# Two-step transposes on VectorE and ScalarE in a hybrid decoder layer on one core

## The chip, the cores and the metric

The kernel runs on one core of one Trainium2 chip, in one launch. The metric is the device time of that launch in microseconds (us). The kernel before takes 1019.77 us, the median of 3 runs (1019.71 to 1019.9).

## The reference, cut to what matters

One decoder layer on 256 tokens with D = 2048, all in float32. What the change touches is the end of it:

```python
def mixer_layer(x, p_i, ...):
    h = rmsnorm(x, norm_g)
    proj = h @ w_in                                   # q, k, v, gate paths, merge gates
    ya = moba_attention(...); yb = swa_attention(...); yc = rglru_branch(...)
    y = jnp.stack([ya * silu(ga), yb * silu(gb), yc * silu(gc)], axis=2)
    y_d = einsum('bsnc,ncd->bsnd', y, w_br)           # each branch to D columns
    gates = sigmoid(mg)
    merged = einsum('bsnd,bsnd->bsd', gates, y_d)     # gated sum of the three branches
    x = x + merged @ w_out
    x = x + sigmoid(rmsnorm(x, ple_norm_g) @ w_pg) * (p_i @ w_pp)
    return x
# output: rmsnorm(x, final_norm_g)
```

A matrix product on TensorE (PE) contracts over partitions, so its left side has to lie feature-major: features on the 128 partitions, tokens along the row. `merged` and the new `x` come out of a product token-major, and both are left sides of the next product (`w_out`, then `w_pg`). They must be transposed on the way.

## The kernel before, in words

**Three products for one.** Every float32 value that goes through PE is split into a rounded high part and the rest (`_hi`, `_lo`). `mm3` (L115 to L119) makes a product out of three matmuls: high by high (L117), high by the weights' low part (L118), low by high (L119).

**Weights.** A weight tile is 128 by 1024 float32 (512 KB). SyncE fetches it into one of 4 raw buffers (`r_*`, L96); `split` (L99) has ScalarE (ACT) cast it into `wh_*` (L111) and VectorE (DVE) subtract that from it into `wl_*` (L112), each in one of 4 buffers. A tile of a 512-column product holds two of the 128-feature steps `k`, and PE makes 2 steps x 2 token halves x 3 = 12 matmuls of 512 columns from it.

**Stages at the end.** `merge` (L634) runs for the three branches in turn; for the last (`bi == 2`, names ending in b) it goes over four column blocks `n`. For each, the gate columns are projected (`ps_in`, 8 weight tiles), then the branch output (`ps_brb`, 4 tiles); DVE multiplies (L647) and adds to `merged` (L648); then `turn` (L620) makes the block feature-major. After that `w_out` runs over four blocks (`ps_out`, 8 tiles each); DVE adds `x` (L673), ACT takes the squares (L676), and `turn` makes the new `x` feature-major as `x2T`, scaled by the norm's gain. Last, `w_pg` runs over blocks of 512 (`ps_pg`; names pg0, pg1, pg2, 8 tiles each) and two of 256 columns; ACT takes the sigmoid from PSUM (L711).

**The transposes.** `turn` has PE transpose 128 by 128 squares against an identity into a PSUM tile `tp_*` (L626), 8 squares for a block of 512 columns and 256 tokens. ACT and DVE then split straight out of that PSUM tile (`split_act`, L179 and L180, or `split_scaled`, L192 and L193). Eight blocks are turned: m0 to m3 of `merged` and x20 to x23 of `x`.

**What sets the order.** A scheduler orders the instructions of each engine from a simulated timeline when the kernel is built; `high_priority` (L105) pulls the splitting of weights ahead of other work, and `tc.issue_after` puts an instruction behind a named one on its engine. On the chip, each engine then works through its own list strictly in that order. A product into PSUM has two buffers (`ps_mm`), small scratch tiles (`temp`) four.

Of the kernel before, what the change touches and what calls it, by code (L numbers as in the profile page):

```python
# [11 lines left out]
F32 = mybir.dt.float32  # L12
# [25 lines left out]
NEG = -1e30  # L38
SLOT = 2112
WPAD = 64  # L40
WOFF = 32
RV = 384

# [2 lines left out]
def trunk(ctx: ExitStack, tc: tile.TileContext, x, xt, p, table, onehot, maskv, w_in, sinks, conv, w_ri, vec, fin, w_br,  # L46
# [23 lines left out]
    def temp(name):  # L70
        return small.tile([P, 4, SEQ], F32, tag="tmp", name=name, bufs=4)
# [14 lines left out]

    raws = {}
    casts = []
    loads = []
    first_parts = {}  # L90

# [7 lines left out]
    def split(name, off):  # L99
        r, pieces = raws.pop(name)  # L100
        hi = wsp.tile([P, WT + WPAD], F32R, tag="whi", name=f"wh_{name}")[:, off : off + WT]
        lo = wsp.tile([P, WT + WPAD], F32R, tag="wlo", name=f"wl_{name}")[:, off : off + WT]
        n = WT // pieces
        part = first_parts.pop(name, None)
        with tc.high_priority(offset=LEAD if part is None else 0):  # L105
            for j in range(pieces):
                c = slice(j * n, (j + 1) * n)
                if part:
                    part(j, pieces)
                with tc.issue_after(casts[-1]) if part else nullcontext():  # L110
                    casts.append(nc.scalar.copy(hi[:, c], r[:, c]).ins)  # L111
                nc.vector.tensor_tensor(lo[:, c], r[:, c], hi[:, c].bitcast(F32), op=ALU.subtract)  # L112
        return hi, lo

    def mm3(ps, a, b, first, last):  # L115
        (ah, al), (bh, bl) = a, b
        nc.tensor.matmul(ps, ah, bh, start=first, stop=False)  # L117
        nc.tensor.matmul(ps, ah, bl, start=False, stop=False)  # L118
        nc.tensor.matmul(ps, al, bh, start=False, stop=last)  # L119

    def weights_of(src, row, name, sub, off=0):
        held = {}

        def get(k):
            s = k // sub
            if s not in held:
                key = f"{name}_{s}"
                if key not in raws:
                    fetch(src, row + s, key)
                held[s] = split(key, off)  # L130
            return held[s], k % sub

        return get

    def matrix_psum(name):
        return ps_mm.tile([P, NH, CW], F32, tag="mm", name=f"ps_{name}")

    def project(act, src, row, name, cw=CW, weights=None, half=None, hooks={}):
        nk = len(act)
        if half is None:  # L140
            ps = matrix_psum(name).rearrange("p h c -> p (h c)")
        else:
            ps = aux(f"ps_{name}_{half}")
        get = weights or weights_of(src, row, name, WT // cw)
        for k in range(nk):
            w, kk = get(k)
            if k in hooks:
                with tc.issue_after(casts[-1]):
                    hooks[k]()
            c = slice(kk * cw, (kk + 1) * cw)  # L150
            for h in range(NH) if half is None else [half]:
                o = h * cw if half is None else 0
                q = slice(h * P, (h + 1) * P)
                mm3(ps[:, o : o + cw], [t[:, q] for t in act[k]], [t[:, c] for t in w],
                    k == 0 and o % CW == 0, k == nk - 1 and (half is not None or (o + cw) % CW == 0))
        return ps if half is not None else ps[:, : NH * cw].rearrange("p (h c) -> p h c", h=NH)

    def project_turned(row, name):
        ps = matrix_psum(name)
# [460 lines left out]
    def turn(u, n, src, name, gain=None):  # L620
        for j in range(0, 4, 2):
            pt = aux(f"tp_{name}{n}{j}")
            for i in range(2):
                for h in range(NH):
                    c = n % 2 * CW + (j + i) * P
                    nc.tensor.transpose(pt[:, i * SEQ + h * P : i * SEQ + (h + 1) * P], src[:, h, c : c + P], ident)  # L626
            k = n % 2 * 4 + j
            if gain is None:
                split_act(u, k, 2, pt)
            else:  # L630
                for i in range(2):
                    split_scaled([t[:, cols(k + i)] for t in u], pt[:, cols(i)], gain[:, 4 * n + j + i : 4 * n + j + i + 1])

    def merge(z, bi, br):  # L634
        if bi == 0:
            merged.extend(wide(block(f"merged{h}")) for h in range(2))
        for n in range(4):
            sg = token_major(temp(f"sg_{br}{n}"))
            ps = in_chunk()
            for h in range(NH):  # L640
                nc.scalar.activation(sg[:, h, :], ps[:, h, :], AF.Sigmoid, scale=rs1[:, h : h + 1])
            py = project(act_of(z), w_br, (bi * 4 + n) * KB * CW // WT, f"br{br}{n}")
            dst = merged[n // 2][:, :, half_cols(n)]
            if bi == 0:
                nc.vector.tensor_tensor(dst, py, sg, op=ALU.mult)
                continue
            nc.vector.tensor_tensor(sg, py, sg, op=ALU.mult)  # L647
            (nc.vector if bi == 2 else nc.gpsimd).tensor_tensor(dst, dst, sg, op=ALU.add)  # L648
            if bi == 2:
                if n % 2 == 0:  # L650
                    mT.append(unit(f"m{n // 2}"))
                turn(mT[n // 2], n, merged[n // 2], "m")

    steps = branch_c()
    next(steps)
# [14 lines left out]
    for n in range(4):  # L670
        ps = project(act_of(*mT), w_out, n * KD * CW // WT, f"out{n}")
        sl = xr[n // 2][:, :, half_cols(n)]
        nc.vector.tensor_tensor(sl, ps, sl, op=ALU.add)  # L673
        junk = token_major(temp(f"jy{n}"))
        for h in range(NH):
            nc.scalar.activation(junk[:, h, :], sl[:, h, :], AF.Square, accum_out=sq2[:, h, n : n + 1])  # L676
        turn(x2T[n // 2], n, xr[n // 2], "x2", ple_g)
    tot = const.tile([P, NH], F32, name="tot")
    rs2 = const.tile([P, NH], F32, name="rs2")
    nc.vector.reduce_sum(tot, sq2, axis=AX.X)  # L680
# [13 lines left out]
    for n in range(5):  # L694
        cw = CW if n < 3 else HW
        at = n * CW if n < 3 else 3 * CW + (n - 3) * HW
        b, lc = at // BW, slice(at % BW, at % BW + cw)
        if n < 3:
            parts = project(act_of(*x2T), w_pg, n * KD * CW // WT, f"pg{n}")
        elif n == 3:  # L700
            parts = project(act_of(*x2T), w_pgt, 0, f"pg{n}", cw=HW)
        y = token_major(temp(f"y{n}"))
        junk = token_major(temp(f"jz{n}"))
        ws = weights_of(w_pgt, KD * HW // WT, f"pg{n}", WT // HW)
        for h in range(NH):
            if n == 4:
                ps = project(act_of(*x2T), None, 0, f"pg{n}", cw=HW, weights=ws, half=h)[:, :HW]
            else:
                ps = parts[:, h, :]
            yh, xh = y[:, h, :cw], xr[b][:, h, lc]  # L710
            nc.scalar.activation(yh, ps, AF.Sigmoid, scale=rs2[:, h : h + 1])  # L711
            nc.vector.tensor_tensor(yh, yh, pps[b][:, h, lc], op=ALU.mult)
            nc.vector.tensor_tensor(xh, xh, yh, op=ALU.add)
            if n < 4:
                nc.scalar.activation(junk[:, h, :cw], xh, AF.Square, accum_out=sq3[:, h, n : n + 1])
                nc.gpsimd.tensor_tensor(xh, xh, fg[:, at : at + cw], op=ALU.mult)
                continue
            t, r = tot3[:, h : h + 1], rs3[:, h : h + 1]
            nc.vector.tensor_tensor_reduce(junk[:, h, :cw], xh, xh, op0=ALU.mult, op1=ALU.add, scale=1.0,
                                           scalar=0.0, accum_out=t)  # L720
            nc.vector.tensor_scalar(t, t, 1.0 / D, part[:, h : h + 1], op0=ALU.mult, op1=ALU.add)
            nc.gpsimd.tensor_tensor(r, t, half_c[:, :1], op=ALU.pow)
            nc.vector.tensor_tensor(xh, xh, fg[:, at : at + cw], op=ALU.mult)
            for eng, c0, c1 in ((nc.sync, 0, BW), (nc.scalar, BW + CW, D), (nc.sync, BW, BW + CW)):
                sl = xr[c0 // BW][:, h, c0 % BW : c0 % BW + c1 - c0]
                if eng is nc.sync:
                    nc.vector.tensor_scalar_mul(sl, sl, r)
                else:
                    nc.scalar.activation(sl, sl, AF.Copy, scale=r)
                eng.dma_start(out[h * P : (h + 1) * P, c0:c1], sl)  # L730
        if n == 3:
            nc.vector.reduce_sum(part, sq3, axis=AX.X)
            nc.vector.tensor_scalar(part, part, 1.0 / D, EPS, op0=ALU.mult, op1=ALU.add)
# [78 lines left out]
```

## Time and profile before

| what | value |
|---|---|
| median of 3 runs | 1019.77 us |
| the profiled execution's own time | 1020.7 us |
| its span on the core | 1018.6 us |
| PE busy, share of the span | 1007.2 us, 99% |
| PE weight loads (PEld) | 857.7 us, 84% |
| DVE busy | 653.6 us, 64% |
| ACT busy | 555.2 us, 55% |
| granted PE clock | 0.998 of full |
| share of the chain that ended last | PE 96%, DMA 2%, issue 1% |

A busy time is the union of an engine's instructions. Matmuls overlap in the pipeline, so what PE needs for a stretch is read from the distances between the starts of its instructions, not from the mean time of one. The chain of waits is followed back from the last instruction; an engine with 96% of it sets the end.

### The profile page before, as it was taken

What the parts mean: (1) busy time and instruction counts of PE and PEld (TensorE: products, weight loads), DVE (VectorE), ACT (ScalarE), POOL (GpSimd) and SP (SyncE); (2) the same over time, 40 slices, a digit from 0 to 9 for tenths busy, and PEclk for the clock granted to TensorE, in tenths of its full rate; (3) what the DMA queues carried; (4) which work ended last, traced back from release to release, by engine and by line L of the source; (5) the groups of instructions that cost most, each with busy time, mean ns of one, the idle gap of its engine ahead of it and who ended that gap; (6) DMA issues with size and microseconds to landing.
All of it is one profiled execution on the core that took longest, in us unless ns stands there. A gap on an engine that the chain in (4) does not pass through costs nothing.

```text
span 1018.6 us, 13635 instructions
## 1 busy us (share of the span) xinstructions
PE 1007.2 (99%) x5152; PEld 857.7 (84%) x5152; DVE 653.6 (64%) x961; ACT 555.2 (55%) x794; POOL 30.4 (3%) x22
## 2 busy tenths in 40 slices
PE   9999999999999999999999999999999999999996
PEld 7788888888888888888988888888888888888886
DVE  5866956667967754465556777767665555555564
ACT  6744445558567554444445756665654444444552
POOL 0000000000000000000000011001000000000122
PEclk9999999999999999999999999999999999999999
DMA  9866655555656555555555565555555665576652
GB/s 331 288 224 211 209 182 184 179 173 165 208 166 196 176 186 187 194 197 188 186 186 179 193 186 176 176 185 185 167 189 187 231 239 170 190 276 221 197 187 83
DMA packets 58200, 199.50 MB, mean 196 GB/s; under 512 B 6600, under 2 KB 10008, under 8 KB 57624
## 3 DMA queue, kind: packets, MB, share of 16 engines
q1 hardware_dynamic: 51840, 186.41, 56.2%
q10 hardware_dynamic: 6296, 12.24, 3.5%
q8 instruction: 40, 0.66, 0.3%
q14 instruction: 24, 0.20, 0.1%
HBM read 194.40 MB, written 4.23 MB: 195 GB/s over the span
## 4 chain that ended last, share of the span: by engine, by line
PE 96%; DMA 2%; issue 1%; DVE 0%; ACT 0%; SPq 0%; POOLq 0%; POOL 0%; ACTq 0%; DVEq 0%
PE ps_in L165 21%; PE ps_in L167 11%; PE ps_in L118 10%; PE ps_in L119 10%; PE ps_in L117 10%; PE ps_out L119 3%; PE ps_out L118 3%; PE ps_out L117 3%; PE ps_pg L117 3%; PE ps_pg L118 3%; PE ps_pg L119 3%; PE ps_bra L118 1%; PE ps_brc L118 1%; PE ps_bra L119 1%; PE ps_bra L117 1%; PE ps_brc L119 1%
## 5 line engine op out<-in xcount | busy, mean ns | idle before, releaser
L112 DVE TENSOR_TENSOR wl_in<-r_in,wh_in 128x1024 fp32r<-128x1024 f32 x232 | 283.3, 1227 | 179.0 <-ACT wh_in L111 178.7
L111 ACT CAST wh_in<-r_in 128x1024 fp32r<-128x1024 f32 x232 | 242.6, 1049 | 253.1 <-PE ps_in L165 140.4
L165 PE MATMUL ps_in<-h,wh_in 128*128 128x512 f32 x928 | 290.2, 393 | 0.0
L167 PEld LDWEIGHTS ps_in<-h,wl_in 128*128 128x128 f32 x928 | 173.5, 188 | 39.3
L118 PE MATMUL ps_in<-wl_in,h 128*128 128x512 f32 (+1 forms) x480 | 184.7, 385 | 0.7 <-DVE wl_in L112 0.7
L167 PE MATMUL ps_in<-h,wl_in 128*128 128x256 f32 x928 | 184.4, 280 | 0.0
L117 PE MATMUL ps_in<-wh_in,h 128*128 128x512 f32 (+1 forms) x480 | 183.9, 383 | 0.0
L119 PE MATMUL ps_in<-wh_in,h 128*128 128x512 f32 (+1 forms) x480 | 183.7, 383 | 0.0
L165 PEld LDWEIGHTS ps_in<-h,wh_in 128*128 128x128 f32 x928 | 142.5, 188 | 0.3
L118 PEld LDWEIGHTS ps_in<-wl_in,h 128*128 128x128 f32 x480 | 90.3, 188 | 19.1 <-DVE wl_in L112 1.5
L117 PEld LDWEIGHTS ps_in<-wh_in,h 128*128 128x128 f32 x480 | 90.3, 188 | 17.4
L119 PEld LDWEIGHTS ps_in<-wh_in,h 128*128 128x128 f32 x480 | 90.3, 188 | 17.0
L112 DVE TENSOR_TENSOR wl_pg<-r_pg,wh_pg 128x1024 fp32r<-128x1024 f32 x32 | 39.8, 1243 | 38.3 <-ACT wh_pg L111 38.3
L112 DVE TENSOR_TENSOR wl_out<-r_out,wh_out 128x1024 fp32r<-128x1024 f32 x32 | 39.2, 1224 | 36.8 <-ACT wh_out L111 36.8
L111 ACT CAST wh_pg<-r_pg 128x1024 fp32r<-128x1024 f32 x32 | 33.7, 1053 | 42.3 <-PE ps_pg L119 35.2
L111 ACT CAST wh_out<-r_out 128x1024 fp32r<-128x1024 f32 x32 | 33.7, 1053 | 42.0 <-PE ps_out L119 36.5
L119 PE MATMUL ps_pg<-wh_pg,x_lo 128*128 128x512 f32 (+1 forms) x160 | 55.4, 347 | 0.0
L118 PE MATMUL ps_pg<-wl_pg,x_hi 128*128 128x512 f32 (+1 forms) x160 | 55.3, 347 | 0.0
L117 PE MATMUL ps_pg<-wh_pg,x_hi 128*128 128x512 f32 (+1 forms) x160 | 55.3, 347 | 0.0
L118 PE MATMUL ps_out<-wl_out,m_hi 128*128 128x512 f32 x128 | 50.1, 391 | 0.0
L117 PE MATMUL ps_out<-wh_out,m_hi 128*128 128x512 f32 x128 | 49.9, 390 | 0.0
L119 PE MATMUL ps_out<-wh_out,m_lo 128*128 128x512 f32 x128 | 49.8, 389 | 0.0
(260 smaller groups left out, 1279.5 us busy)
## 6 DMA issues: line engine op xcount, KB each, us to landing
r_in<-w_in_dram SPq DMA_DIRECT2D x232, 512.0 KB, 3.5
r_out<-w_out_dram SPq DMA_DIRECT2D x32, 512.0 KB, 4.2
r_pg<-w_pg_dram SPq DMA_DIRECT2D x24, 512.0 KB, 4.2
r_brc<-w_br_dram SPq DMA_DIRECT2D x16, 512.0 KB, 3.4
r_bra<-w_br_dram SPq DMA_DIRECT2D x16, 512.0 KB, 3.9
r_brb<-w_br_dram SPq DMA_DIRECT2D x16, 512.0 KB, 3.5
r_pg<-w_pgt_dram SPq DMA_DIRECT2D x8, 512.0 KB, 3.4
x<-xt_dram SPq DMA_DIRECT2D x4, 512.0 KB, 7.2
```

The lines of the kernel that those rows point to most:

```text
L111: casts.append(nc.scalar.copy(hi[:, c], r[:, c]).ins)
L112: nc.vector.tensor_tensor(lo[:, c], r[:, c], hi[:, c].bitcast(F32), op=ALU.subtract)
L117: nc.tensor.matmul(ps, ah, bh, start=first, stop=False)
L118: nc.tensor.matmul(ps, ah, bl, start=False, stop=False)
L119: nc.tensor.matmul(ps, al, bh, start=False, stop=last)
L165: nc.tensor.matmul(ps[:, j, :], wh[:, cs[j]], h_both[k], start=k == 0, stop=False)
L167: nc.tensor.matmul(ps[:, j, SEQ:], wl[:, cs[j]], h_act[k][0], start=False, stop=k == KD - 1)
```

## The change

Seven of the eight blocks (m0, m1, m2, x20 to x23) go through a new function `turn_later`; m3 stays with `turn`. For a block of 128 x 1024 (two token halves of 512 columns):

- Step one: one DVE transpose over the whole block (`t0`, L665 of the changed kernel), which turns each 32 by 32 square in place of its own 32 partitions.
- Step two: 16 pieces of 32 partitions x 256 values that bring the squares to their rows in `t1`. Ten are ACT copies out of `t0` (L671); six are DVE transposes straight from the source (L673).
- Then the split into high and low part, out of `t1` in SBUF instead of `tp` in PSUM.

The 16 pieces are put on a list two by two, and the split as a ninth entry. `tick`, called each time a weight tile is split, takes one entry off the list. Since the last block x23 is then spread over nine weight tiles, `project_two` takes pg0 and pg1 by turns: 12 steps `k` (6 tiles) of pg0, 6 tiles of pg1, then the last 2 tiles of each, which are the ones that read x23.

```diff
+    los = []
+    todo = []
...
-                nc.vector.tensor_tensor(lo[:, c], r[:, c], hi[:, c].bitcast(F32), op=ALU.subtract)
+                los.append(nc.vector.tensor_tensor(lo[:, c], r[:, c], hi[:, c].bitcast(F32), op=ALU.subtract).ins)
         return hi, lo
+
+    def tick():
+        if todo:
+            for on_scalar, work in todo.pop(0):
+                with tc.issue_after((casts if on_scalar else los)[-1]):
+                    work()
...
                 held[s] = split(key, off)
+                tick()
...
+    def project_two(act, src, names, late):
+        pss = [matrix_psum(n) for n in names]
+        gets = [weights_of(src, i * KD * CW // WT, n, WT // CW) for i, n in enumerate(names)]
+        for ks in (range(late), range(late, KD)):
+            for ps, get in zip(pss, gets):
+                for k in ks:
+                    w, kk = get(k)
+                    c = slice(kk * CW, (kk + 1) * CW)
+                    for h in range(NH):
+                        q = slice(h * P, (h + 1) * P)
+                        mm3(ps[:, h], [t[:, q] for t in act[k]], [t[:, c] for t in w], k == 0, k == KD - 1)
+        return pss
...
+    quad = [slice(i * QD, (i + 1) * QD) for i in range(P // QD)]
+
+    def turn_later(u, n, src, name, gain=None):
+        t1, t2 = (temp(f"t{i}_{name}{n}") for i in range(2))
+        k = n % 2 * 4
+        piece = src[:, :, n % 2 * CW : (n % 2 + 1) * CW]
+        s, d = (t.rearrange("p j q -> p (j q)") for t in (t1, t2))
+        s = s.rearrange("p (h c) -> p h c", h=NH)
+        nc.vector.transpose(s, piece)
+
+        def move(i, f, q):
+            to = d[quad[f]].rearrange("p (j h q) -> p h j q", h=NH, j=4)[:, :, :, quad[q]]
+            of = (s if i else piece)[quad[q]].rearrange("p h (j f) -> p h j f", j=4)[:, :, :, quad[f]]
+            if i:
+                nc.scalar.copy(to, of)
+            else:
+                nc.vector.transpose(to, of)
+
+        def finish():
+            if gain is None:
+                split_act(u, k, 4, d)
+            else:
+                for i in range(4):
+                    split_scaled([o[:, cols(k + i)] for o in u], t2[:, i, :], gain[:, 4 * n + i : 4 * n + i + 1])
+
+        on_scalar = [1, 1, 1, 0, 1, 0, 1, 1, 1, 0, 1, 0, 1, 0, 1, 0]
+        blocks = [(f, q) for f in range(4) for q in range(4)]
+        work = [(i, lambda i=i, b=b: move(i, *b)) for i, b in zip(on_scalar, blocks)]
+        todo.extend(work[c : c + 2] for c in range(0, 16, 2))
+        todo.append([(1, finish)])
...
-                turn(mT[n // 2], n, merged[n // 2], "m")
+                (turn_later if n < 3 else turn)(mT[n // 2], n, merged[n // 2], "m")
...
-        turn(x2T[n // 2], n, xr[n // 2], "x2", ple_g)
+        turn_later(x2T[n // 2], n, xr[n // 2], "x2", ple_g)
...
-        if n < 3:
+        if n == 0:
+            two = project_two(act_of(*x2T), w_pg, ["pg0", "pg1"], KD - 4)
+        if n < 2:
+            parts = two[n]
+        elif n == 2:
             parts = project(act_of(*x2T), w_pg, n * KD * CW // WT, f"pg{n}")
```

How the lists of the engines change at the places that matter:

ACT, where block m0 is turned, during the product `ps_brb1`; in216 are the weight tiles of the gate product after it. Before:

```order
L111 CAST wh_brb1_3_6700<-r_brb1_3_6698 128x1024
L641 ACT_TABLE_LOAD
L641 ACTIVATE sg_b1_6495<-ps_in208_6496,rs_in_512 128x512 x2
L111 CAST wh_in216_0_6736<-r_in216_0_6734 128x1024
L179 CAST m0_hi_6479<-tp_m00_6481 128x512
L179 CAST m0_hi_6479<-tp_m02_6488 128x512
L111 CAST wh_in216_1_6754<-r_in216_1_6752 128x1024
```

and after:

```order
L114 CAST wh_brb1_3_6707<-r_brb1_3_6705 128x1024
L671 COPY t1_m0_6482<-t0_m0_6481 32x2x4x32 x10
L695 ACT_TABLE_LOAD
L695 ACTIVATE sg_b1_6484<-ps_in208_6485,rs_in_512 128x512 x2
L114 CAST wh_in216_0_6732<-r_in216_0_6730 128x1024
L202 CAST m0_hi_6479<-t1_m0_6482 128x1024
L114 CAST wh_in216_1_6752<-r_in216_1_6750 128x1024
```

All ten copies stand in one run ahead of the table load, the sigmoid and the cast of the first tile of in216, although the list hands them out two by two.

DVE at the same place, before:

```order
L648 TENSOR_TENSOR merged0_2957<-merged0_2957,sg_b0_6256 128x2x512
L112 TENSOR_TENSOR wl_brb1_2_6683<-r_brb1_2_6680,wh_brb1_2_6682 128x1024
L112 TENSOR_TENSOR wl_brb1_3_6701<-r_brb1_3_6698,wh_brb1_3_6700 128x1024
L112 TENSOR_TENSOR wl_in216_0_6737<-r_in216_0_6734,wh_in216_0_6736 128x1024
L180 TENSOR_TENSOR m0_lo_6480<-tp_m00_6481,m0_hi_6479 128x512
```

and after:

```order
L702 TENSOR_TENSOR merged0_2957<-merged0_2957,sg_b0_6256 128x2x512
L115 TENSOR_TENSOR wl_brb1_2_6690<-r_brb1_2_6687,wh_brb1_2_6689 128x1024
L665 STREAM_TRANSPOSE t0_m0_6481<-merged0_2957 128x1024
L673 STREAM_TRANSPOSE t1_m0_6482<-merged0_2957 32x2x4x32 x6
L115 TENSOR_TENSOR wl_brb1_3_6708<-r_brb1_3_6705,wh_brb1_3_6707 128x1024
L115 TENSOR_TENSOR wl_in216_0_6733<-r_in216_0_6730,wh_in216_0_6732 128x1024
L203 TENSOR_TENSOR m0_lo_6480<-t1_m0_6482,m0_hi_6479 128x1024
```

The full transpose and the six pieces stand between the low parts of two weight tiles of the running product.

DVE at the end of block x23 (wl_pg are the low parts of the w_pg tiles, in the order in which PE takes them). Before:

```order
L112 TENSOR_TENSOR wl_pg0_5_7996<-r_pg0_5_7993,wh_pg0_5_7995 128x1024
L193 SCALAR_TENSOR_TENSOR x21_lo_7217<-tp_x230_7869,vecs_89,x21_hi_7216 128x256
L193 SCALAR_TENSOR_TENSOR x21_lo_7217<-tp_x232_7878,vecs_89,x21_hi_7216 128x256
L193 SCALAR_TENSOR_TENSOR x21_lo_7217<-tp_x230_7869,vecs_89,x21_hi_7216 128x256
L193 SCALAR_TENSOR_TENSOR x21_lo_7217<-tp_x232_7878,vecs_89,x21_hi_7216 128x256
L112 TENSOR_TENSOR wl_pg0_6_8014<-r_pg0_6_8011,wh_pg0_6_8013 128x1024
```

and after:

```order
L673 STREAM_TRANSPOSE t1_x23_7906<-xr1_7230 32x2x4x32
L115 TENSOR_TENSOR wl_pg1_4_8133<-r_pg1_4_8131,wh_pg1_4_8133 128x1024
L673 STREAM_TRANSPOSE t1_x23_7906<-xr1_7230 32x2x4x32
L115 TENSOR_TENSOR wl_pg1_5_8154<-r_pg1_5_8151,wh_pg1_5_8153 128x1024
L216 SCALAR_TENSOR_TENSOR x21_lo_7238<-t1_x23_7906,vecs_89,x21_hi_7237 128x256 x4
L115 TENSOR_TENSOR wl_pg0_6_8180<-r_pg0_6_8177,wh_pg0_6_8179 128x1024
```

Here the pieces do alternate with the tiles. The finished block x23 stands behind the twelfth tile (pg1_5) and ahead of the thirteenth (pg0_6), the first that is multiplied with it. On PE nothing moves but this: the 56 transposes are gone, and the 24 matmuls of pg0's last two tiles stand behind pg1's sixth. The loads of `pp0`, `pp1` and `fg` (1 MB each, on ACT's queue) move from the time of out3's sixth weight tile to that of out2's second.

## Rows read from the trace of the kernel before

**Rows 1.** The page: busy time by engine, and the chain that ended last by engine.

```profile
PE 1007.2 (99%) x5152; PEld 857.7 (84%) x5152; DVE 653.6 (64%) x961; ACT 555.2 (55%) x794; POOL 30.4 (3%) x22
...
PE 96%; DMA 2%; issue 1%; DVE 0%; ACT 0%; SPq 0%; POOLq 0%; POOL 0%; ACTq 0%; DVEq 0%
```

**Rows 2.** All waits of PE: line, waited for, us in total, times, longest.

```profile
PE busy L261 <- DVE sp L352: 1.1, 1, 1.1
PE ps_in L118 <- DVE wl_in L112: 0.7, 1, 0.7
PE ps_pp L117 <- ACT wh_pp L111: 0.6, 1, 0.6
```

**Rows 3.** Timeline of PE around block m0: start, length, instruction, count.

```profile
753.19 0.39 PE L118 MATMUL ps_brb<-wl_brb,zb_hi 128*128 128x512 f32 x1
...
754.78 0.39 PE L119 MATMUL ps_brb<-wh_brb,zb_lo 128*128 128x512 f32 x1
755.01 1.03 PE L626 MATMUL tp_m<-ident,merged 128*128 128x128 f32 x8
755.80 0.48 PE L117 MATMUL ps_brb<-wh_brb,zb_hi 128*128 128x512 f32 x1
756.11 0.40 PE L118 MATMUL ps_brb<-wl_brb,zb_hi 128*128 128x512 f32 x1
...
759.30 0.39 PE L117 MATMUL ps_brb<-wh_brb,zb_hi 128*128 128x512 f32 x1
...
762.70 0.39 PE L117 MATMUL ps_in<-wh_in,h 128*128 128x512 f32 x1
```

**Rows 4.** The chain in order of time: first and last of eight transpose groups.

```profile
755.17 0.87 PE tp_m L626 x8
...
926.44 0.87 PE tp_x L626 x8
```

**Rows 5.** Timeline of ACT around block m0; in brackets idle time before, and releaser.

```profile
751.12 1.05 ACT L111 CAST wh_brb<-r_brb 128x1024 fp32r<-128x1024 f32 x1 [1.66 <-PE ps_in L119]
752.20 1.28 ACT L641 ACT_TABLE_LOAD   x1
753.49 1.27 ACT L641 ACTIVATE sg_b<-ps_in,rs_in 128x512 f32<-128x512 f32 x2
754.65 1.05 ACT L111 CAST wh_in<-r_in 128x1024 fp32r<-128x1024 f32 x1
...
760.18 1.05 ACT L111 CAST wh_in<-r_in 128x1024 fp32r<-128x1024 f32 x1 [1.66 <-PE ps_brb L119]
762.90 1.06 ACT L111 CAST wh_in<-r_in 128x1024 fp32r<-128x1024 f32 x1 [1.67 <-PE ps_brb L119]
```

**Rows 6.** Timeline of DVE around block m0.

```profile
750.52 1.22 DVE L112 TENSOR_TENSOR wl_brb<-r_brb,wh_brb 128x1024 fp32r<-128x1024 f32 x1
752.21 1.23 DVE L112 TENSOR_TENSOR wl_brb<-r_brb,wh_brb 128x1024 fp32r<-128x1024 f32 x1 [0.47 <-ACT wh_brb L111]
...
761.26 1.22 DVE L112 TENSOR_TENSOR wl_in<-r_in,wh_in 128x1024 fp32r<-128x1024 f32 x1 [1.49 <-ACT wh_in L111]
```

**Rows 7.** Groups of ACT by line and form: busy us, mean ns of one, idle before.

```profile
L471 ACT ACTIVATE e_a<-e_a,st0a 128x256 f32<-128x256 f32 x8 | 4.0, 500 | 0.0
L539 ACT CAST k_b<-kvb 64x256 fp32r<-64x256 f32 x4 | 1.6, 404 | 0.1
```

**Rows 8.** Groups of DVE by line and form.

```profile
L193 DVE SCALAR_TENSOR_TENSOR x_lo<-tp_x,vecs,x_hi 128x256 fp32r<-128x256 f32 x16 | 7.0, 478 | 0.6 <-ACT x_hi L192 0.6
L573 DVE TENSOR_TENSOR y_b<-py_b,y_b 64x256 f32<-64x256 f32 x16 | 6.7, 420 | 2.5 <-ACT y_b L571 2.4
L449 DVE TENSOR_TENSOR_SCAN xcT<-rg,ig 128x256 f32<-128x256 f32 x8 | 4.9, 671 | 0.0
L727 DVE TENSOR_SCALAR xr<-xr,rs 128x1024 f32<-128x1024 f32 x2 | 1.5, 754 | 0.9 <-POOL rs L722 0.9
```

**Rows 9.** Timeline of ACT just after pg0.

```profile
944.18 1.26 ACT L711 ACTIVATE y<-ps_pg,rs 128x512 f32<-128x512 f32 x2
```

**Rows 10.** One wait of ACT for a weight load, from 740 to 1015 us.

```profile
ACT wh_pg L111 <- DMA r_pg<-w_pg_dram: 3.4, 2, 2.3
```

More of the change, by code (lines that the diff above doesn't have):

```diff
@@ L40 @@
 WPAD = 64
+QD = 32
 WOFF = 32
```

## Prediction

> **What bounds the kernel now.** I read the page's busy times and its chain first, then PE's waits, then the timelines at the place where the most work lands at once. PE is busy for 99% of the span and holds 96% of the chain that ended last [rows 1]. The reader is to see that the other engines can only matter through PE waiting for them, and in the whole span PE does so three times, for 2.4 us together [rows 2], all of them outside the stages that change. So two questions decide: how much time PE loses on the transposes, and whether the work that replaces them makes a weight tile late.
>
> **How much cover a weight tile has.** In the steady state ACT casts a tile every 2.72 us (760.18 to 762.90), and each cast waits for PE to release the buffer used four tiles earlier [rows 5]. A tile is 12 matmuls, so one takes PE 0.2267 us. When a cast can start, PE still has three tiles to go, 8.16 us. Cast and low part take from 760.18 to 762.48 (761.26 plus 1.22), 2.30 us [rows 5, 6]. The slack is 8.16 - 2.30 = 5.86 us: ACT and DVE together may make a tile that much late before PE notices.
>
> **Removed: 56 transposes on PE.** From the matmul at 753.19 to the one at 759.30 lie 6.11 us and 23 pitches, with eight transposes between [rows 3]. 23 x 0.2267 is 5.21, so one group costs 0.90 us. The chain gives 0.87 for it, at all eight places within 0.01 [rows 4]; the difference is the two matmuls just behind, which start slowly (755.80 to 756.11). Seven of the eight groups go: 7 x 0.87 = 6.1 to 7 x 0.90 = 6.3. I take 6.2 us.
>
> The Trainium skill, page "VectorE: DVE Perf Modes", section "The three transpose paths", gives 390 ns for a 128 by 128 transpose on TensorE and 311 ns on VectorE (2-byte values). By 390 ns, 56 transposes would be an estimated 21.8 us; the trace has eight in a row at 0.87 us, 0.11 each, and decides.
>
> **Added on ACT and DVE, seven times.** The copies are 32 x 256 values from SBUF to SBUF; the nearest row is the cast of 64 x 256 at 404 ns, and above it stand the 128 x 256 exponentials at 500 [rows 7]. I take 0.404, so ten are 4.0 us, up to 5.0. No DVE transpose stands in the trace. For the full one I take the subtraction of the same 128 x 1024, 1.23 us [rows 6]; below it is the 0.754 of a multiplication by a scalar, above it four times the slowest row of 256 elements (a scan, 0.671), 2.68 [rows 8]. For a piece I take 0.420, up to 0.671 [rows 8]; six are 2.5 us, up to 4.0. The splits read SBUF instead of PSUM and count as before.
>
> In the products behind x20 to x23, a round of 8 tiles lasts 21.76 us. DVE then needs 8 x 1.23, one addition of the same size, 1.22, 4 x 0.478 for the low parts [rows 8], 1.23 and 2.52 for the transposes: 16.7 us. ACT has 8 x 1.05, ten copies of 4.0, four activations at up to 0.500 and two squares of half a cast's width, each shorter than one: below 16.6. Both fit, so on average the added work lies beside the matmuls and costs nothing.
>
> **The tight place: m0.** Here the scheduler put all ten copies in one run ahead of a table load, a sigmoid and the cast of the first tile of in216. In steps: the low part at 750.52 ends at 751.74 [rows 6]; the full transpose ends at 752.97; ten copies end at 757.01; the table load (1.28) at 758.29; the sigmoid holds ACT for 1.16 (753.49 to 754.65) [rows 5], to 759.45; the cast ends at 760.50; the low part at 761.72, with some 0.1 of handovers at 761.8. PE wants that tile at 762.70 less the 0.90 of the removed group, 761.80 [rows 3], and its low part one matmul later, 762.03. It arrives 0.2 us early, so I cost it at nothing; but this edge has no cover left. With both upper ends, 1.45 more for the full transpose and 0.96 for the copies, it is 2.2 us late, and PE idles for that. Lower ends give nothing, since PE can't run ahead.
>
> At the other six blocks one to eight copies stand ahead of a cast: 3.2 us at m1, at most 4.0 plus 1.45 for a slow full transpose, inside 5.86. Only where a second delay meets them is there a price. The loads of pp0, pp1 and fg (3 MB) move to x21's time. Where they are now, the longest wait of ACT for a weight load is 2.3 us [rows 10], without any wait of PE. With x21's six copies that makes 2.3 + 2.4 = 4.7, covered; with upper ends 2.3 + 3.0 + 1.45 = 6.75, 0.9 us too late.
>
> **pg0 and pg1 by turns.** The order of 24 matmuls changes, not their number. The first tile that needs x23 is the thirteenth, 32.6 us after pg0 starts. The split of x23 stands behind the twelfth tile's cast, which can start when the eighth tile is done (21.8), and takes 1.05 + 4 x 0.500 + 0.478: 25.3, 7.3 us early. pg2 reuses pg0's PSUM buffer, which is complete after the fourteenth tile; pg2 starts after the sixteenth, 5.44 us later. The sigmoid of pg0 stands behind one cast and takes 1.26 [rows 9]: 2.3 us. Nothing is lost in either.
>
> **Sum.** The profiled execution took 1020.7 us with a span of 1018.6. 1020.7 - 6.2 = 1014.5, a span of 1012.4. The median of the runs is 0.93 below the profiled one, so I forecast 1019.77 - 6.2 = 1013.6 us.
>
> **Rivals.**
> - *One or two tiles late.* The burst at m0 (up to 2.2 us) and x21 with the moved loads (up to 0.9) give back up to 3.1: 1013.8 to 1016.7, about 1015 in the middle. For it: m0's margin of 0.2 us on a path of seven steps, one of which no row shows. Against: my values are taken without the overlap that neighbours show (two sigmoids of 1.27 hold ACT for 1.16) [rows 5].
> - *The gain is given back.* Seven late tiles of 0.6 us or more, about one for each block: 1018 to 1020. For it: each block does bring its run of copies. Against: 5.86 us of cover at six of the seven places.
> - *DVE becomes the bound: slower.* If a transpose of 4-byte values runs at a quarter of the rate of a subtraction, the transposes of a block take 4 x 3.75 = 15.0 us, and DVE needs 16.7 - 3.75 + 15.0 = 27.9 in a round of 21.76. Over four rounds that is 24.8 too much, less 5.86 of cover 18.9, less the 6.2 gained: 12.7 slower, 1032 us. It turns to a loss where (13.0 + 3.75 f - 21.76) x 4 passes 12.1, at f = 3.1 times my value. For it: the operation is in no row. Against: the slowest row per element, the scan, is 1.6 times my value. The same page's section "Rules for kernel authors" sends a 128 by 128 transpose to TensorE where PSUM will do, a rule against this change. No run so far shows the DVE side. From its 311 ns, eight squares would be an estimated 2.5 us for the first step, which would be the rival of late tiles and not this one.
> - That the transposes stay is ruled out: PE's list has 8 left of 64.
>
> **How the numbers follow.** The forecast (1013.0 to 1014.2, from the two readings of a group and some 0.3 of handovers) has 0.66; late tiles 0.18; given back 0.06; DVE as the bound 0.10. About 0.2% (2 us) is what a measurement of this kernel can tell from no change: faster, below 1017.7, has 0.66 + 0.18 = 0.84; within, 0.06; slower 0.10. The range takes the forecast and the late tiles, 1012.9 to 1016.8.
>
> **What would show it.** Right: one `tp_m` group left on PE and no `tp_x`; PE's busy time and span both about 6.2 less; no wait of PE on `wl_in`, `wl_out` or `wl_pg`; the full transposes near 1.2 us, pieces and copies near 0.4. The first tile of in216 shows how close m0 was. Wrong: waits of PE on `wl_in` behind m0, on `wl_out` behind x21; full transposes above 2.7 us; DVE without idle time between 850 and 950 us.

## The result and the profile after

The changed kernel takes 1013.85 us, the median of 5 runs (1012.68 to 1016.7), against 1019.9 for 5 runs of the kernel before: a ratio of 0.994, 95% interval 0.9927 to 0.9954. The forecast was 1013.6. The profiled execution took 1013.85 us with a span of 1012.1; before it was 1020.7 and 1018.6.

The page of the changed kernel, the two rows that answer to [rows 1]:

```profile
PE 1001.0 (99%) x5096; PEld 851.6 (84%) x5096; DVE 680.8 (67%) x1007; ACT 582.7 (58%) x861; POOL 29.0 (3%) x22
...
PE 96%; DMA 2%; issue 1%; DVE 0%; ACT 0%; SPq 0%; POOLq 0%; POOL 0%; ACTq 0%; DVEq 0%
```

PE has 56 instructions and 6.2 us of busy time fewer. DVE has 27.2 us more, ACT 27.5, and yet PE holds 96% of the chain as before. The added work, 54.7 us, is nearly nine times as long as the removed work, and none of it shows in the end.

All waits of PE in the changed kernel, to be laid beside [rows 2]:

```profile
PE busy L284 <- DVE sp L375: 1.1, 1, 1.1
PE ps_in L127 <- DVE wl_in L115: 0.7, 1, 0.7
PE ps_pp L126 <- ACT wh_pp L114: 0.5, 2, 0.3
```

They are the same three rows as before, 2.3 us together, and all of it lies in the first 28 us of the program. No wait on `wl_out` or `wl_pg` has come.

The groups of the new operations by line and form, with the one group of transposes that PE keeps (count, then busy us and mean ns of one):

```profile
L671 ACT COPY t_x<-t_x 32x256 f32<-32x256 f32 x40 | 16.1, 403 | 1.1 <-DVE tot L734 0.4
...
L673 DVE STREAM_TRANSPOSE t_x<-xr 32x256 f32<-32x256 f32 x24 | 10.5, 438 | 0.7
L665 DVE STREAM_TRANSPOSE t_x<-xr 128x1024 f32<-128x1024 f32 x4 | 4.9, 1237 | 0.0
...
L649 PE MATMUL tp_m<-ident,merged 128*128 128x128 f32 x8 | 1.0, 272 | 0.0
```

The values taken were 0.404 for a copy, 0.420 for a piece on DVE and 1.23 for a full transpose. Measured are 0.403, 0.438 and 1.237. The transpose in no row of before costs what the subtraction of the same size costs [rows 6].

Busy times of two of the stretches in which x20 to x23 are turned (length, then PE, PEld, DVE, ACT, POOL; then the granted clock, the DMA share and GB/s):

```profile
850.00:872.00 22.00, 22.00 (x99) 18.22 (x98) 16.45 (x21) 15.55 (x27) 0.00 (x0) 1.00 0.73 263
...
894.00:916.00 22.00, 22.00 (x99) 18.23 (x98) 15.36 (x20) 15.55 (x27) 0.00 (x0) 1.00 0.61 192
```

PE is busy throughout, DVE for 16.45 of 22 us and ACT for 15.55. Worked out beforehand were 16.7 and below 16.6 in 21.76.

**The tight place.** Block m0 in the changed kernel, first ACT, then DVE, then PE (start, length, instruction, count; idle time before and its releaser in brackets):

```profile
752.67 4.15 ACT L671 COPY t_m<-t_m 32x256 f32<-32x256 f32 x10 [0.80 <-DVE t_m L665]
756.83 1.28 ACT L695 ACT_TABLE_LOAD   x1
758.13 1.27 ACT L695 ACTIVATE sg_b<-ps_in,rs_in 128x512 f32<-128x512 f32 x2
759.28 1.04 ACT L114 CAST wh_in<-r_in 128x1024 fp32r<-128x1024 f32 x1
```

```profile
751.34 1.24 DVE L665 STREAM_TRANSPOSE t_m<-merged 128x1024 f32<-128x1024 f32 x1
752.61 2.69 DVE L673 STREAM_TRANSPOSE t_m<-merged 32x256 f32<-32x256 f32 x6
...
760.36 1.23 DVE L115 TENSOR_TENSOR wl_in<-r_in,wh_in 128x1024 fp32r<-128x1024 f32 x1 [3.80 <-ACT wh_in L114]
```

```profile
761.49 0.39 PE L126 MATMUL ps_in<-wh_in,h 128*128 128x512 f32 x1
761.71 0.43 PE L127 MATMUL ps_in<-wl_in,h 128*128 128x512 f32 x1
761.98 0.39 PE L128 MATMUL ps_in<-wh_in,h 128*128 128x512 f32 x1
```

The low part ends at 761.59 and its reader starts at 761.71: 0.12 us early, where 0.2 was forecast. In the runs below where PE does wait for such a low part, it starts 0.06 us after the end, so the cover that was left is about 0.06. The next matmul follows after 0.27 in place of 0.227, so 0.04 us was lost here at most. Most of the missing margin is in the ten copies: 4.15 for a run, 0.415 each, a little more than their length.

**x23 and the moved loads.** In the changed kernel, ACT around the split of x23:

```profile
937.70 1.71 ACT L215 ACTIVATE x_hi<-t_x,vecs 128x256 fp32r<-128x256 f32 x4
939.46 1.06 ACT L114 CAST wh_pg<-r_pg 128x1024 fp32r<-128x1024 f32 x1
```

The four low parts on DVE start at 938.97 and take 1.67, so they end at 940.64. The cast at 939.46 belongs to the thirteenth tile, and it comes at the steady pace of 2.72. PE then has three tiles to go, 8.16, and reaches the thirteenth at 947.62. The split is 7.0 us early; 7.3 was forecast. The longest wait of ACT for a load of `w_out` is 0.8 us, with `pp0`, `pp1` and `fg` moved there:

```profile
ACT wh_out L114 <- DMA r_out<-w_out_dram: 1.4, 2, 0.8
```

**Where the 6 us came from.** The start of the program differs by up to 1.6 us from execution to execution, before anything that changed: in all the traces the first `ps_in` matmul of one line (L165 in the kernel before) starts between 63.4 and 65.1 us, and the cast named next follows it by 679.6 to 679.7 us. To take this out I measure from one fixed point ahead of m0, ACT's cast of the first tile of the running product, to the end of the span. The cast in the trace of before:

```profile
744.37 1.05 ACT L111 CAST wh_brb<-r_brb 128x1024 fp32r<-128x1024 f32 x1 [1.67 <-PE ps_in L119]
```

And in that of the changed kernel:

```profile
744.05 1.05 ACT L114 CAST wh_brb<-r_brb 128x1024 fp32r<-128x1024 f32 x1 [1.67 <-PE ps_in L128]
```

Before: 1018.6 - 744.37 = 274.23. After: 1012.1 - 744.05 = 268.05. That is 6.18 less, for seven groups 0.88 each. This "tail" is used below for every run. It is read from one traced execution of each kernel, and the span has one decimal, so a tail is good to some 0.05; where two kernels should not differ, their tails below agree within 0.11.

### The profile page after: what moved, and what is told of

Read it like the earlier page. It is cut to its first block, busy times and chain, and to the rows that moved or that the text cites. A ratio compares the mean times of both kernels' runs of the same rounds, so it can differ in the third digit from the quotient of the medians.

```text
span 1012.1 us, 13635 instructions
## 1 busy us (share of the span) xinstructions
PE 1001.0 (99%) x5096; PEld 851.6 (84%) x5096; DVE 680.8 (67%) x1007; ACT 582.7 (58%) x861; POOL 29.0 (3%) x22
## 4 chain that ended last, share of the span: by engine, by line
PE 96%; DMA 2%; issue 1%; DVE 0%; ACT 0%; SPq 0%; POOLq 0%; POOL 0%; ACTq 0%; DVEq 0%
PE ps_in L188 21%; PE ps_in L190 11%; PE ps_in L127 10%; PE ps_in L128 10%; PE ps_in L126 10%; PE ps_out L126 3%; PE ps_out L128 3%; PE ps_out L127 3%; PE ps_pg L126 3%; PE ps_pg L127 3%; PE ps_pg L128 3%; PE ps_bra L128 1%; PE ps_bra L127 1%; PE ps_brc L128 1%; PE ps_bra L126 1%; PE ps_brc L127 1%
```

## Experiments

| kernel | median us | ratio to before, 95% interval | start of the cast | span | tail | against before |
|---|---|---|---|---|---|---|
| changed kernel | 1013.85 | 0.994 (0.9927 to 0.9954) | 744.05 | 1012.1 | 268.05 | -6.18 |
| only x20 to x23 | 1015.8 | 0.996 (0.9945 to 0.9975) | 743.28 | 1013.9 | 270.62 | -3.61 |
| only m0 to m2 | 1017.54 | 0.9974 (0.9964 to 0.9983) | 744.21 | 1015.8 | 271.59 | -2.64 |
| only the turns of pg0, pg1 | 1020.41 | 1.0005 (0.9995 to 1.0014) | 743.05 | 1017.2 | 274.15 | -0.08 |
| plain pg order | 1013.74 | 0.9941 (0.9927 to 0.9956) | 743.86 | 1011.8 | 267.94 | -6.29 |
| all eight blocks | 1012.69 | 0.9929 (0.9912 to 0.9945) | 743.31 | 1010.4 | 267.09 | -7.14 |
| all eight, plain pg order | 1012.49 | 0.993 (0.9915 to 0.9945) | 744.67 | 1011.8 | 267.13 | -7.10 |
| m0: 4 copies more | 1015.24 | 0.9956 (0.994 to 0.9972) | 743.08 | 1012.9 | 269.82 | -4.41 |
| m0: 7 copies more | 1017.9 | 0.9973 (0.9962 to 0.9984) | 743.83 | 1016.4 | 272.57 | -1.66 |
| m0: 10 copies more | 1020.88 | 1.0014 (1.0004 to 1.0023) | 743.47 | 1018.0 | 274.53 | +0.30 |
| DVE transposes of x twice | 1013.53 | 0.9933 (0.9919 to 0.9947) | 743.90 | 1011.9 | 268.00 | -6.23 |
| the same, four times | 1035.43 | 1.0156 (1.014 to 1.0171) | 743.40 | 1032.9 | 289.50 | +15.27 |

### The change in parts

Only the blocks of `x`; `merged` is turned on PE as before:

```diff
-                (turn_later if n < 3 else turn)(mT[n // 2], n, merged[n // 2], "m")
+                turn(mT[n // 2], n, merged[n // 2], "m")
```

> Only x20 to x23 go through the new function, m0 to m3 are turned on PE as before; pg0 and pg1 by turns as in the changed kernel. Theory (the gain is PE time of the transposes alone, 0.87 to 0.90 us a group): four groups less, 3.5 to 3.6 us below the kernel before, 1016.3 us; 32 tp_m left, no tp_x. Rival (the gain comes with the order of pg0 and pg1, or from loads that moved): the whole 6.2 us here, 1013.7. Second rival (the work on DVE and ACT is paid for in part): less than 2.5 us.

Only m0 to m2; `x` on PE, and pg0 and pg1 one after the other:

```diff
-        turn_later(x2T[n // 2], n, xr[n // 2], "x2", ple_g)
+        turn(x2T[n // 2], n, xr[n // 2], "x2", ple_g)
...
-        if n == 0:
-            two = project_two(act_of(*x2T), w_pg, ["pg0", "pg1"], KD - 4)
-        if n < 2:
-            parts = two[n]
-        elif n == 2:
+        if n < 3:
             parts = project(act_of(*x2T), w_pg, n * KD * CW // WT, f"pg{n}")
```

> Only m0 to m2 go through the new function; x20 to x23 are turned on PE, and pg0, pg1, pg2 follow each other as before. Theory: three groups less, 2.6 to 2.7 us below the kernel before, 1017.2 us, with a wait of PE of at most 0.2 us for the first tile of in216. Rival (the order of pg0 and pg1 carries the gain): no change, 1019.9. Second rival (m0's burst costs PE a wait): 1.5 us below at most.

Only the turns of pg0 and pg1; both calls of `turn_later` become `turn`:

> All eight blocks are turned on PE as before; only pg0 and pg1 are taken by turns. Theory: the same 24 matmuls in another place, within 0.3 us of the kernel before in the span from the first m0 transpose to the end, 1019.9 us. Rival (the order itself gives something, for instance because the pg tiles meet fewer loads): 1 us or more below.

Four groups of transposes are worth 3.61 us (0.90 each), three 2.64 (0.88), and 3.61 + 2.64 = 6.25 is the 6.18 of the whole within 0.1. The turns alone are worth 0.08, no more than two tails of like kernels differ by. So the gain is the PE time of the transposes, with nothing else larger than 0.1 us, and the parts don't disturb each other.

### Plain order of pg, and all eight blocks

The turns give x23 time. Here pg0 and pg1 run one after the other, and the sixteen pieces of x23 are handed out eight per weight tile:

```diff
-    def turn_later(u, n, src, name, gain=None):
+    def turn_later(u, n, src, name, gain=None, by=2):
...
-        todo.extend(work[c : c + 2] for c in range(0, 16, 2))
+        todo.extend(work[c : c + by] for c in range(0, 16, by))
...
-        turn_later(x2T[n // 2], n, xr[n // 2], "x2", ple_g)
+        turn_later(x2T[n // 2], n, xr[n // 2], "x2", ple_g, by=2 if n < 3 else 8)
```

> The changed kernel without the turns of pg0 and pg1: pg0, pg1, pg2 follow each other as before, and x23's pieces are handed out eight to a tile, so that its split stands behind pg0's seventh tile. Theory (the chain from the addition of x to the last low part of x23 takes some 11 us, and pg0 reads x23 16.3 us after it starts): no wait, the time of the changed kernel, 1013.9 us. Rival (the turns are what keeps PE fed): PE waits 2 us or more for x21_hi or x21_lo, 1016 us or more.

The tail is 267.94 against 268.05: the same. The turns aren't needed if x23's pieces come faster.

All eight blocks, m3 with four pieces per tile:

```diff
-                (turn_later if n < 3 else turn)(mT[n // 2], n, merged[n // 2], "m")
+                turn_later(mT[n // 2], n, merged[n // 2], "m", by=2 if n < 3 else 4)
```

> The changed kernel with m3 also taken off PE, its 16 pieces handed out four to a tile, so that the split stands behind the fifth tile of out0; out0 reads m3 from its seventh tile on. Theory (each group is worth 0.87 to 0.90 us as long as a tile has slack): 0.9 us below the changed kernel, 1012.9 us, no PE transposes of merged left. Rival (the chain through DVE, ACT and DVE takes longer than the six tiles, 16.3 us, that out0 gives it): PE waits for m1_hi or m1_lo and the time is 1 us or more above the changed kernel.

Its page, and the full transposes of its `merged` blocks (ns: least, median, most; first and last start):

```profile
PE 999.8 (99%) x5088; PEld 850.2 (84%) x5088; DVE 684.5 (68%) x1013; ACT 586.5 (58%) x870; POOL 29.0 (3%) x22
...
L665 DVE STREAM_TRANSPOSE t_m<-merged x4: 1234/1240/1246, 750.6 to 829.8; 128x1024 f32<-128x1024 f32 x4
```

The eighth group is gone, and PE doesn't wait at `w_out` for m3, which starts at 829.8. The tail is 0.96 shorter than the changed kernel's, one more group.

Both together:

> All eight blocks through the new function (m3 four pieces to a tile, x23 eight) and the w_pg blocks one after the other. Theory: no PE transposes of merged or x, no wait, 0.9 us below the changed kernel, 1012.9 us, the same as with all eight and the turns. Rival (bursts of m3 and x23 add up with the moved loads): 1 us or more above that.

These two are the fastest, by 1.2 and 1.4 us in the medians. Their intervals against before overlap with the changed kernel's, so that they beat it rests on the tails (267.09 and 267.13 against 268.05).

### What a late tile costs

The rival of late tiles had at most 0.12 us between it and the truth. Here ten more copies stand at m0, ahead of the sigmoid and the cast as the ten do now:

```diff
-                with tc.issue_after(casts[-1]) if part else nullcontext():
+                with tc.issue_after(casts[-1] if part else hold[-1]) if part or name == "in216_0" else nullcontext():
...
             if i:
-                nc.scalar.copy(to, of)
+                for _ in range(2 if (name, n) == ("m", 0) else 1):
+                    hold[:] = [nc.scalar.copy(to, of).ins]
...
-                nc.scalar.activation(sg[:, h, :], ps[:, h, :], AF.Sigmoid, scale=rs1[:, h : h + 1])
+                with tc.issue_after(hold[-1]) if (bi, n) == (2, 1) else nullcontext():
+                    sig = nc.scalar.activation(sg[:, h, :], ps[:, h, :], AF.Sigmoid, scale=rs1[:, h : h + 1]).ins
+                if (bi, n) == (2, 1):
+                    hold[:] = [sig]
```

> The changed kernel with each of the ten ACT copies of block m0 issued twice (the same values again), and ACT's order at that place held as in the changed kernel: copies, table load, sigmoid, cast of in216's first tile. Theory (m0 is the one place without cover: the low part of that tile came 0.1 us before PE wanted it): the ten extra copies, 4.15 us, show nearly whole as one wait of PE on wl_in or wh_in, 4.0 us above the changed kernel, 1017.9 us. Rival (the four weight buffers still cover such a delay, 5.86 us in the steady state): no wait, 1013.9 us.

The wait came as expected, but the loss was larger: the tail is 274.53 - 268.05 = 6.48 longer than the changed kernel's. The twenty copies took 8.53 us, 4.38 more than the ten (4.15 was expected):

```profile
752.09 8.53 ACT L673 COPY t_m<-t_m 32x256 f32<-32x256 f32 x20 [0.81 <-DVE t_m L666]
```

PE around the wait, and then the busy times of the stretch (line numbers are one higher here; the last figures are the granted clock, the DMA share and GB/s):

```profile
760.68 0.39 PE L129 MATMUL ps_brb<-wh_brb,zb_lo 128*128 128x512 f32 x1
764.18 0.79 PE L127 MATMUL ps_in<-wh_in,h 128*128 128x512 f32 x1 [3.11 <-ACT wh_in L115]
765.44 0.79 PE L128 MATMUL ps_in<-wl_in,h 128*128 128x512 f32 x1 [0.47 <-DVE wl_in L116]
766.03 0.63 PE L129 MATMUL ps_in<-wh_in,h 128*128 128x512 f32 x1
766.46 0.63 PE L127 MATMUL ps_in<-wh_in,h 128*128 128x512 f32 x1
```

```profile
762.00:764.00 2.00, 0.00 (x0) 0.00 (x0) 0.00 (x0) 2.00 (x3) 0.00 (x0) 0.83 0.00 0
764.00:766.00 2.00, 1.35 (x2) 0.79 (x3) 1.84 (x2) 2.00 (x4) 0.00 (x0) 0.50 0.00 0
766.00:768.00 2.00, 2.00 (x6) 1.58 (x5) 2.00 (x3) 1.91 (x3) 0.00 (x0) 0.50 0.77 236
768.00:770.00 2.00, 2.00 (x6) 1.52 (x6) 2.00 (x3) 0.00 (x0) 0.00 (x0) 0.50 0.70 227
770.00:772.00 2.00, 2.00 (x10) 1.68 (x9) 2.00 (x2) 1.05 (x1) 0.00 (x0) 0.96 0.86 268
```

While PE idles the granted clock falls to 0.50, the lower of its two levels (1.2 GHz), and stays there until 770 although PE works again from 764.18. Matmuls follow each other by 0.43 us in place of 0.227. How late PE is, the distances between starts tell: the second matmul of `ps_in` starts 4.76 us after the last of `ps_brb` (760.68 to 765.44) where two pitches are 0.45, so it is 4.31 late. The missing 6.48 - 4.31 = 2.17 us is the slow clock: 4.7 us of work from 765.44 to 770.1 at 0.43 in place of 0.227 lose 2.2.

Does every wait bring this? The same kernel with only the first four or the first seven of the ten copies done twice, and the sigmoid held behind all of them:

```diff
-                for _ in range(2 if (name, n) == ("m", 0) else 1):
-                    hold[:] = [nc.scalar.copy(to, of).ins]
+                for _ in range(2 if (name, n) == ("m", 0) and (f, q) <= (1, 0) else 1):
+                    hold.append(nc.scalar.copy(to, of).ins)
```

With seven the bound is (2, 0) in place of (1, 0).

> Block m0 is copied with 14 ACT copies in place of ten (four of them done twice), all ahead of the sigmoid and the cast of in216's first tile. Four copies at the pitch of 0.415 us are 1.66 late, less 0.1 of cover: PE waits about 1.5 us at that tile. Theory 1: a wait this short costs only itself, the granted clock stays at 1.00 behind it: 1013.85 + 1.5 = 1015.4 us. Theory 2: the clock falls behind this wait as it did behind the one of 3.5 us, for about 6 us: 1015.4 + 3 = 1018.4 us, and the rows show 0.50 between 763 and 769.

> The same with 17 copies (seven done twice): 2.9 us late, less 0.1: PE waits about 2.8 us. Theory 1 (only the wait counts up to here): 1013.85 + 2.8 = 1016.7 us with a clock of 1.00. Theory 2 (the clock falls behind it): 1016.7 + 3 = 1019.7 us, 0.50 for some 6 us. If the run with 14 copies keeps its clock and this one doesn't, the price of a late tile jumps between waits of 1.5 and 2.8 us.

The copies of the two runs on ACT, first with four more, then with seven:

```profile
751.70 5.90 ACT L673 COPY t_m<-t_m 32x256 f32<-32x256 f32 x14 [0.81 <-DVE t_m L666]
752.45 7.22 ACT L673 COPY t_m<-t_m 32x256 f32<-32x256 f32 x17 [0.81 <-DVE t_m L666]
```

PE with four more, and its clock behind the wait:

```profile
760.29 0.39 PE L129 MATMUL ps_brb<-wh_brb,zb_lo 128*128 128x512 f32 x1
761.16 0.50 PE L127 MATMUL ps_in<-wh_in,h 128*128 128x512 f32 x1 [0.48 <-ACT wh_in L115]
762.42 0.50 PE L128 MATMUL ps_in<-wl_in,h 128*128 128x512 f32 x1 [0.76 <-DVE wl_in L116]
762.76 0.40 PE L129 MATMUL ps_in<-wh_in,h 128*128 128x512 f32 x1
```

```profile
762.00:764.00 2.00, 1.58 (x7) 1.30 (x8) 2.00 (x3) 2.00 (x4) 0.00 (x0) 1.00 0.35 63
```

PE with seven more, and its clock:

```profile
761.04 0.39 PE L129 MATMUL ps_brb<-wh_brb,zb_lo 128*128 128x512 f32 x1
763.23 0.50 PE L127 MATMUL ps_in<-wh_in,h 128*128 128x512 f32 x1 [1.80 <-ACT wh_in L115]
764.49 0.79 PE L128 MATMUL ps_in<-wl_in,h 128*128 128x512 f32 x1 [0.76 <-DVE wl_in L116]
```

```profile
764.00:764.50 0.50, 0.01 (x1) 0.01 (x1) 0.50 (x2) 0.50 (x2) 0.00 (x0) 0.73 0.00 0
764.50:765.00 0.50, 0.50 (x1) 0.49 (x2) 0.50 (x1) 0.50 (x2) 0.00 (x0) 0.50 0.00 0
...
767.50:768.00 0.50, 0.50 (x3) 0.36 (x3) 0.50 (x2) 0.00 (x0) 0.00 (x0) 0.85 0.72 221
```

| copies more | added on ACT | second matmul of `ps_in` late by | tail against the changed kernel | of it beyond the lateness | clock at 0.50 |
|---|---|---|---|---|---|
| 4 | 1.75 | 1.68 | +1.77 | 0.1 | no |
| 7 | 3.07 | 3.00 | +4.52 | 1.5 | 764.2 to 767.7 |
| 10 | 4.38 | 4.31 | +6.48 | 2.2 | 763.3 to 770.1 |

(Added on ACT is the length of the copies less 4.15. Late by is read from the starts in the rows, as above; the waits in brackets count from the ends, which are modelled, and come to less. The last column is worked out from the clocks of the windows.) In all three runs PE is 0.07 us less late than the copies are longer, which is the cover once more. With four more copies only the lateness counts, as the first theory had it; with seven the clock falls, but for a shorter time than the second theory expected (1017.9 where it had 1019.7). So the price of being late isn't a straight line: 1.7 us late cost 1.8, 4.3 us late cost 6.5. The medians say the same: 1015.24, 1017.9 and 1020.88 against 1013.85.

### How much room DVE has

The DVE transposes of x20 to x23 issued four times:

```diff
-        nc.vector.transpose(s, piece)
+        for _ in range(4 if name == "x2" else 1):
+            nc.vector.transpose(s, piece)
...
-                nc.vector.transpose(to, of)
+                for _ in range(4 if name == "x2" else 1):
+                    nc.vector.transpose(to, of)
```

> The changed kernel with every DVE transpose of x20 to x23 issued four times (the same values again), as if it ran at a quarter of its rate; the scheduler spreads the extra ones over the lists. Theory (DVE has room for the transposes as they are and not for four times that): DVE needs 28.6 us for a round of 21.76 in out1 to out3, 6.8 too much, three rounds 20, less 5.9 of cover: PE waits for wl_out, wl_pg or x20 and x21 for some 14 us, 1028 us, between 1020 and 1036. Rival (DVE work of this kind stays hidden also then): 1013.9 us.

The waits of PE that have come:

```profile
PE ps_pg L127 <- DVE wl_pg L115: 7.6, 4, 5.4
PE ps_out L127 <- DVE wl_out L115: 5.2, 2, 3.2
PE ps_pg L126 <- ACT x_hi L215: 2.0, 1, 2.0
```

and one of its stretches (columns as above):

```profile
860.00:870.00 10.00, 10.00 (x46) 8.28 (x45) 9.53 (x17) 7.97 (x14) 0.00 (x0) 1.00 0.48 154
```

DVE is busy for 9.53 of 10 us, so it has become the bound, and PE waits 14.8 us, 12.8 of them for DVE itself. The tail is 21.45 longer than the changed kernel's, and 1035.43 lies in the range that was expected, 7 above its middle. Part of the 6.7 that the waits leave over is the clock again, as a stretch behind the longest wait shows:

```profile
940.00:950.00 10.00, 8.10 (x25) 6.38 (x26) 9.59 (x18) 2.84 (x6) 0.71 (x1) 0.66 0.49 159
```

The same twice in place of four times:

> The DVE transposes of blocks x20 to x23 are issued twice in place of once. Theory (DVE becomes the bound only above about three times the price): DVE has 13.0 + 2 x 3.8 = 20.6 us of work in a round of 21.76, so PE doesn't wait for it: 1013.85 us, at most 0.5 more. Rival (every added DVE operation delays a low part that PE wants): the seven extra operations of a block are 3.8 us, four blocks 15 us, 1020 us or more with PE waiting on wl_out and wl_pg.

```profile
894.00:916.00 22.00, 22.00 (x99) 18.22 (x98) 20.47 (x28) 15.59 (x27) 0.00 (x0) 1.00 0.64 210
```

DVE has 20.47 of 22 us, PE is busy throughout, and the tail is the changed kernel's (268.00 against 268.05). So the room ends between two and four times the price; the rival that every added DVE operation delays PE is out.

## Why the prediction was right, and where it was not

- **The sum.** Removed were 7 x 0.88 = 6.18 us by the tails, 0.87 to 0.90 a group by [rows 3, 4]. Nothing was given back. The forecast of 1013.6 is 0.25 below the median.
- **The prices from neighbouring rows** held within 5%: copies by the cast of 64 x 256 [rows 7], the full transpose by the subtraction [rows 6], the pieces by the rows of 256 elements [rows 8]. The upper ends (0.500, 2.68, 0.671) were far off. For the two on DVE this was in part luck: no row of before had a transpose there, so nothing but the like shape spoke for the price.
- **Transposes belong on TensorE.** The Trainium skill, page "VectorE: DVE Perf Modes", section "Rules for kernel authors", sends a 128 by 128 transpose to TensorE if a PSUM destination will do. Here that costs 0.88 us a block and the other way nothing, since PE is 99% busy and DVE and ACT are not. The result goes against the rule, and the measurement decides for this kernel.
- **The tight place** was named rightly and lay at 0.12 us of cover instead of 0.2, with 0.04 lost at most. That it held was luck as well: the ten copies alone took 0.11 more than their price, about as much as the cover that was left.
- **x23, pg2 and the moved loads** cost nothing, as worked out; x23 was 7.0 us early.
- **DVE as the bound.** The break-even at 3.1 times lies between the two points measured, with no loss at twice and a loss at four times. The price of that rival for four times, 1032 us, was 3.4 below the 1035.43 measured; it too counted no slower clock.
- **The step that failed** stands in the rival of late tiles: "it is 2.2 us late, and PE idles for that". PE's idle time is not the whole price. The runs show 1.8 us for 1.7 late, but 4.5 for 3.0 and 6.5 for 4.3, because the clock falls with the wait and stays low behind it. The 2.2 us, between 1.7 and 3.0, would have cost from 1.8 to 4.5, and with the 0.9 at x21 the rival would have reached 1016.3 to 1019.0 in place of 1016.7. The upper end of the range, 1016.8, was too low for that; it did no harm only because no tile was late.

Two things stay open. Single runs lie up to 2.9 us above the median of the changed kernel (1016.7), up to 3.9 above that of the kernel before (1023.82), and one of the ten runs with only the turns took 2614.91 us (the median of the other nine is 1020.24); no trace of such a run was taken. And what sets the 1.6 us of difference in the first 65 us of the program wasn't looked into.

## What to carry to other kernels

Where one engine is busy for 99% and the others for two thirds, work moved off it paid its full PE time here though it takes nine times as long elsewhere, as long as each weight tile stayed inside its cover; count that cover place by place and not on average. A place with 0.1 us of cover held in every trace of a kernel with ten copies at m0, but being late has two prices: the wait itself, and in two of the three sizes tried a slower clock for several us behind it. For an operation that no row shows, the row of the same shape on the same engine gave the best price here; the far bounds belong in the range.

## What the hardware showed that was not expected

- The granted clock of TensorE fell to 0.50 (1.2 GHz) within a wait of 3.11 us and stayed there until 770.1, 5.9 us after work had resumed; with waits of 1.80 and 0.76 us it was at 0.50 for 3.4 us; with 0.48 and 0.76 it stayed at 1.00.
- A transpose of 128 x 1024 4-byte values on DVE took 1.237 us, no more than a subtraction of that size (1.23); of 32 x 256 it took 0.438, and an ACT copy of the same shape 0.403, 0.415 from one to the next.
